# A two-layer decoder trunk in split float32 products: first loads from one queue, squares summed on VectorE, another order for the output product's last units, and a scale spread by two float32r products

## The chip, the cores and the metric

The kernel runs on one core of one Trainium2 chip, in one launch. The metric is the device time of one execution in microseconds (us). Three executions of the kernel before took 1090.64 to 1091.21 us, the median 1091.2.

## What is computed

The input is one sequence of 512 positions with 1024 features, in float32. Two layers follow each other. Each has a token mixer and a gated MLP, both behind an RMSNorm, both added to the residual `h`:

```python
def rmsnorm(x, g):
    y = xf * lax.rsqrt(jnp.mean(xf * xf, axis=-1, keepdims=True) + RMS_EPS)
    return y * g
# layer 0: z = gelu(h @ w_in); u, v = split(z); v = layernorm(v);
#          s = causal 128x128 mixing of v in each chunk + b_s;   mix = (u * s) @ w_out
# layer 1: q, k, v, f_logit = split(h @ w_qkvf); causal softmax attention in 16 heads of 64,
#          logits + cumulative log-sigmoid forget gates;         mix = o @ w_o
# both:    a = conv_b + causal depthwise conv3(h @ w_gate);  h + (silu(a) * (h @ w_up)) @ w_down
# last:    rmsnorm(h, final_norm_g)
```

The weights are about 90 MB of float32 and are read once.

## The kernel before

**Units.** All weights lie in memory as units of 128 x 1024 float32 (512 KB), in the order of use. `fetch` (lines 75 to 83) asks SP for the next unit into one of three `raw` buffers and calls `split` (lines 110 to 113): ACT casts the unit to float32r, the high half `whi` (line 112), and DVE subtracts that from the unit, the low half `wlo` (line 113). There are two buffers each of `whi` and `wlo`. `unit(depth)` keeps up to `depth` units fetched ahead and hands out the oldest. Activations are split in the same way into `x` or `z` pairs.

**Products.** A block of 128 x 128 weights by 512 positions is three float32r matrix products into one PSUM bank (`triple`, lines 165 to 169: high by high, high by low, low by high). A unit is 8 blocks, so 24 products. PSUM has eight banks: two each under the tags g, s, a and b. The kernel is one stream of such products on PE; a tile scheduler has set each engine's order from the order in which the code is written, and within an engine instructions run in that order.

**Norms.** `norm_split` (lines 115 to 130) scales a 128-feature block of `h` by the norm's weight and splits it, so the products can begin before the norm's scale is known. `norm_square` (lines 132 to 141) squares the block on ACT and adds the square to a running sum on POOL (line 141). `norm_end` sums over partitions by four one-column products (line 148), takes the inverse root on DVE with three Newton steps (lines 96 to 108) on a 128 x 4 tile, and multiplies the identity by each of its columns into a 128 x 512 tile of four diagonals (line 152). `norm_spread` (line 159) multiplies that by a matrix of ones in plain float32, which spreads the scale to all partitions. This happens for four norms; the last norm of the kernel is done in another way in the tail.

**The start.** `build` first runs nine small float32 products of ones (line 742, 18 passes on PE), and loads the first weights from SP (lines 751 and 78) and the input `x` from ACT's queue (lines 745 to 754), so that ACT's first casts stand behind its own DMA instructions. The first unit is loaded and split in two pieces of 512 columns.

**The output product of the attention.** `wo` multiplies the attention's result (pairs `z`) by eight units of w_o, (group, half) = (0,0) (1,0) (2,0) (0,1) (1,1) (2,1) (3,0) (3,1). A group is two PSUM banks of 128 output features; the banks of the groups 0, 1, 2 are gg, ab, ss. Each half holds four blocks of 128 input features, and the last of these (two heads) is ready only when the attention ends. So the (0,1) and (1,1) units are held in the two `whi`/`wlo` buffers, all their products but those with the last block are issued, then the last ones, and the buffers come free for (2,1). After each group `add_to_h` adds its banks to `h` (line 216) and does the next norm's `norm_split` and `norm_square`. The attention's probabilities are split into three buffers with the tag `hl`.

Of the kernel before, what the change touches and what calls it, by code (L numbers as in the profile page):

```python
# [8 lines left out]
F32 = mybir.dt.float32  # L9
F32R = mybir.dt.float32r  # L10
# [3 lines left out]
ALU = mybir.AluOpType  # L14
AX = mybir.AxisListType

P = 128
T = 512
D = 1024
KD = D // P  # L20
# [3 lines left out]
NT = T // P  # L24
# [8 lines left out]
V_MIX = 0  # L33
# [9 lines left out]
class Trunk:  # L43
# [29 lines left out]


    def fetch(self):
        nc = self.nc
        raw = self.sb("raw", 3, [P, 1024])
        nc.sync.dma_start(out=raw, in_=self.ins["w"][self.iu])
        self.iu += 1
        hi = self.sb("whi", 2, [P, 1024], F32R)  # L80
        lo = self.sb("wlo", 2, [P, 1024], F32R)
        self.split(hi, lo, raw)
        self.ahead.append((hi, lo))

    def unit(self, depth=2):

# [45 lines left out]
    def norm_square(self, k):  # L132

        nc = self.nc
        if self.acc is None:
            self.acc = self.tmp()
            nc.scalar.activation(out=self.acc, in_=self.h[k], func=AF.Square)
        else:
            sq = self.tmp()
            nc.scalar.activation(out=sq, in_=self.h[k], func=AF.Square)  # L140
            nc.gpsimd.tensor_tensor(out=self.acc, in0=self.acc, in1=sq, op=ALU.add)  # L141

    def norm_end(self):

        nc = self.nc
        pt = self.ps("a")
        for i in range(NT):
            nc.tensor.matmul(pt[:, i : i + 1], self.acc[:, i * P : (i + 1) * P], self.ones[:, 0:1], start=True, stop=True)
        self.r4 = self.rsqrt(pt[:, 0:NT], NT, 1.0 / D, RMS_EPS)
        dg = self.tmp()  # L150
        for i in range(NT):
            nc.vector.tensor_scalar(out=dg[:, i * P : (i + 1) * P], in0=self.ident, scalar1=self.r4[:, i : i + 1],
                                    scalar2=None, op0=ALU.mult)
        self.dg = dg

    def norm_spread(self):
        nc = self.nc
        pb = self.ps("b")
        nc.tensor.matmul(pb, self.ones, self.dg, start=True, stop=True)
        self.R = self.sb("R", 1, [P, T])  # L160
        nc.scalar.copy(out=self.R, in_=pb)

# [200 lines left out]
    def fox(self):  # L363
        nc = self.nc
        V = [self.sb("v", 4, [P, H, P], F32R) for _ in range(NT)]
        self.V = V
        x = (self.xh, self.xl)

        wf3 = self.wfr.rearrange("p (k h) -> p k h", k=KD)
        self.wf = self.sb("pt", 3, [P, 1280], F32R)[:, 0:1024].rearrange("p (k c) -> p k c", k=KD)  # L370
        nc.gpsimd.memset(self.wf.bitcast(F32), 0.0)
        hi, lo = self.wf[:, :, 0:H], self.wf[:, :, H : 2 * H]
        nc.gpsimd.tensor_copy(out=hi, in_=wf3)
        nc.gpsimd.tensor_tensor(out=lo, in0=wf3, in1=hi.bitcast(F32), op=ALU.subtract)

        def each_v(g, kp):
            if g == 0 and kp == 2:
                self.norm_end()
            elif g == 0 and kp == 3:
                self.norm_spread()  # L380
                self.gates()
            elif g == 1 and kp == 1:
                self.running_sums()

        def evac_v(g, banks):
            for i in range(NT):
                r = self.r4[:, i : i + 1]
                src = banks[i].rearrange("p (h d) -> p h d", d=HD)
                vh, vl = V[i][:, 8 * g : 8 * g + 8, 0:HD], V[i][:, 8 * g : 8 * g + 8, HD:P]
                nc.scalar.activation(out=vh, in_=src, func=AF.Copy, scale=r)  # L390
                nc.vector.scalar_tensor_tensor(out=vl, in0=src, scalar=r, in1=vh.bitcast(F32), op0=ALU.mult, op1=ALU.subtract)

        self.gemm_tm(x, KD, 2, evac_v, each_v)

        self.oh, self.ol = [], []
        self.st, self.pr, self.hl, self.po = {}, {}, {}, {}

        def qk():
            for p in range(H // 2):
                st = self.stack_tiles(p)  # L400
                pq, pk = self.ps("g"), self.ps("g")
                for u in range(2):
                    hi, lo = self.unit()
                    for m, pt in enumerate((pq, pk)):
                        for j in range(4):
                            k = 4 * u + j
                            c = slice(j * 256 + m * P, j * 256 + (m + 1) * P)
                            self.triple(pt, (hi[:, c], lo[:, c]), (x[0][k], x[1][k]), k == 0, k == KD - 1)
                            if k == KD - 1:
                                (self.stack_k if m else self.stack_q)(p, pt, st)  # L410
                            yield

        def wo():

            y = (self.oh, self.ol)
            evac = self.add_to_h(V_FFN + 8, 2)
            banks = {}

            def blocks(g, unit, half, ks):
                hi, lo = unit  # L420
                for m in range(2):
                    for j in ks:
                        k = 4 * half + j
                        c = slice(j * 256 + m * P, j * 256 + (m + 1) * P)
                        self.triple(banks[g][m], (hi[:, c], lo[:, c]), (y[0][k], y[1][k]), k == 0, k == KD - 1)
                        yield

            for g, tags in enumerate(("gg", "ab", "ss")):
                banks[g] = [self.ps(tag) for tag in tags]
                yield from blocks(g, self.unit(), 0, range(4))  # L430
            held = []
            for g in range(2):
                held.append(self.unit(2 - g))
                yield from blocks(g, held[g], 1, range(3))
            for g in range(2):
                yield from blocks(g, held[g], 1, (3,))
                evac(g, banks[g])
            yield from blocks(2, self.unit(), 1, range(4))
            evac(2, banks[2])
            banks[3] = [self.ps("g") for _ in range(2)]  # L440
            for half in range(2):
                yield from blocks(3, self.unit(), half, range(4))
            evac(3, banks[3])

        def products():
            yield from qk()
            yield from wo()

        gen = products()
        for _ in range(20):
            next(gen)
        for slot in range(4 * H + LAG):
            for _ in range(2):
                next(gen)
            self.attend(slot)
        self.run(gen)
# [235 lines left out]

    def constants(self):
        nc = self.nc
        nc.gpsimd.affine_select(out=self.ident, in_=self.ones, pattern=[[1, P]], compare_op=ALU.is_equal, fill=0.0,
                                base=0, channel_multiplier=-1)
        nc.gpsimd.affine_select(out=self.tri, in_=self.ones, pattern=[[1, P]], compare_op=ALU.is_ge, fill=0.0,
# [4 lines left out]
                                base=0, channel_multiplier=1)  # L704
        nc.gpsimd.tensor_copy(out=self.identb, in_=self.ident)
        nc.gpsimd.tensor_copy(out=self.maskb, in_=mask)
        nc.sync.dma_start(out=self.wfr, in_=self.ins["wf"])
        nc.gpsimd.tensor_copy(out=self.fold, in_=self.ident[0 : 2 * H, 0:H])
        nc.gpsimd.tensor_tensor(out=self.fold, in0=self.fold, in1=self.ident[0 : 2 * H, H : 2 * H], op=ALU.add)
        self.cum = self.sb("cum", 1, [P, T], F32R)  # L710
# [4 lines left out]
    def build(self):  # L715
        nc, tc = self.nc, self.tc
        with tc.tile_pool(name="sb", bufs=1) as self.pool, \
                tc.tile_pool(name="ps", bufs=1, space=bass.MemoryType.PSUM) as self.psum:
            self.ones = self.sb("ones", 1, [P, P])
            self.ident = self.sb("ident", 1, [P, P])  # L720
            self.tri = self.sb("tri", 1, [P, P])
            self.wfr = self.small(P, tag="wfr", bufs=1)
            self.vec = self.sb("vec", 1, [P, NV])
            self.identb = self.sb("identb", 1, [P, P], BF16)
            self.maskb = self.sb("maskb", 1, [P, P], BF16)
# [19 lines left out]
            nc.scalar.dma_start(out=self.vec, in_=self.ins["vec"])  # L745
            raw = self.sb("raw", 3, [P, 1024])
            hi, lo = self.sb("whi", 2, [P, 1024], F32R), self.sb("wlo", 2, [P, 1024], F32R)

            for j in range(2):
                c = slice(j * 512, (j + 1) * 512)  # L750
                nc.sync.dma_start(out=raw[:, c], in_=self.ins["w"][0, :, c])
                nc.scalar.dma_start(out=hb[0][:, j], in_=self.ins["x"][:, j])
            for q in range(1, KD // 2):
                nc.scalar.dma_start(out=hb[q], in_=self.ins["x"][:, 2 * q : 2 * q + 2])
            for j in range(2):
                c = slice(j * 512, (j + 1) * 512)
                self.split(hi[:, c], lo[:, c], raw[:, c])
                self.norm_split(j, V_MIX, 2)
            self.iu = 1
            self.ahead.append((hi, lo))  # L760
            self.fetch()
            for k in range(2, KD):
                self.norm_split(k, V_MIX)

            self.gmlp()
            self.run(self.gemm_fm((self.zh, self.zl), KE, 2, self.add_to_h(V_FFN)))
# [71 lines left out]
```

## Time and profile before

| | |
|---|---|
| median of three runs | 1091.2 us (1090.64 to 1091.21) |
| the profiled execution's own time | 1091.33 us |
| its span, first to last instruction | 1089.6 us |
| PE busy | 1074.4 us (99%), 5018 instructions |
| DVE, ACT, POOL busy | 622.1, 441.5, 70.4 us |
| mean granted TensorE clock | 0.994 of full speed |

The time of an execution is the span and a further 1.7 us around it. PE is the engine that bounds the kernel: a moment without a product, or with products at the lower of TensorE's two clock levels (1.2 GHz rather than 2.4 GHz), lengthens the span, while idle time on another engine costs nothing by itself. A matrix product's row shows its start and its pipelined duration (0.39 us); the next one starts 0.2275 us after it at full clock, and 0.43 us after it at the lower level, so the distance between starts is what counts.

### The profile page before, as it was taken

The numbers are of one execution on the slowest core, as the hardware profiler recorded it, in microseconds if no ns is written. First come the engines' busy times: TensorE is split into PE (matmuls) and PEld (weight loads), VectorE is DVE, ScalarE is ACT, GpSimd is POOL, SyncE is SP. The second block draws the span as 40 slices with busy tenths as digits, with TensorE's granted clock in tenths as the row PEclk, the third lists the DMA queues.
The fourth block names the chain that finished last, engine by engine and source line by source line (L and its number), as shares of the span: only waits on it lengthen the run. The fifth ranks groups of instructions, "written<-read, shape, count | busy, mean of one in ns | idle before, by whom it ended". The sixth has DMA issues, their size and how long they took to land.

```text
span 1089.6 us, 12928 instructions
## 1 busy us (share of the span) xinstructions
PE 1074.4 (99%) x5018; PEld 885.5 (81%) x5018; DVE 622.1 (57%) x1007; ACT 441.5 (41%) x706; POOL 70.4 (6%) x62
## 2 busy tenths in 40 slices
PE   8999999999999999999999999999989999999997
PEld 7878888888888888888887888877768888888886
DVE  5535856534555665545254699999564655655242
ACT  6332333322333433333133577777442433433232
POOL 5000000001200000001020010110030000000000
PEclk9999999999999999999999999999989999999999
DMA  6222222222223222222222211111122223232222
GB/s 257 96 79 96 93 82 78 96 98 96 98 78 97 97 97 97 99 96 98 97 96 83 98 61 41 60 62 59 59 78 97 95 97 98 78 116 78 97 97 78
DMA packets 28669, 99.44 MB, mean 91 GB/s; under 512 B 3456, under 2 KB 3712, under 8 KB 28608
## 3 DMA queue, kind: packets, MB, share of 16 engines
q1 hardware_dynamic: 27744, 96.42, 25.7%
q10 hardware_dynamic: 864, 2.20, 0.5%
q8 instruction: 39, 0.64, 0.2%
q14 instruction: 22, 0.18, 0.1%
HBM read 96.12 MB, written 2.10 MB: 90 GB/s over the span
## 4 chain that ended last, share of the span: by engine, by line
PE 89%; DVE 7%; ACT 2%; DMA 1%; issue 1%; ACTq 0%; DVEq 0%
PE psg L167 11%; PE psg L168 11%; PE psg L169 11%; PE pss L169 9%; PE pss L167 9%; PE pss L168 9%; PE psa L167 4%; PE psa L168 4%; PE psa L169 4%; PE psb L167 4%; PE psb L168 4%; PE psb L169 4%; DVE wlo L113 2%; DVE hl L113 1%; DVE z L545 1%; PE psa L590 1%
## 5 line engine op out<-in xcount | busy, mean ns | idle before, releaser
L113 DVE TENSOR_TENSOR wlo<-raw,whi 128x1024 fp32r<-128x1024 f32 (+1 forms) x173 | 219.6, 1269 | 371.4 <-ACT whi L112 359.2
L112 ACT CAST whi<-raw 128x1024 fp32r<-128x1024 f32 (+1 forms) x173 | 180.8, 1045 | 453.0 <-PE psg L168 132.2
L167 PE MATMUL psg<-x,whi 128*128 128x512 f32 x336 | 136.1, 405 | 0.0
L169 PE MATMUL psg<-x,wlo 128*128 128x512 f32 x336 | 131.3, 391 | 0.0
L168 PE MATMUL psg<-x,whi 128*128 128x512 f32 x336 | 130.9, 390 | 0.0
L167 PE MATMUL pss<-x,whi 128*128 128x512 f32 x192 | 75.9, 395 | 0.0
L168 PE MATMUL pss<-x,whi 128*128 128x512 f32 x192 | 74.7, 389 | 0.0
L169 PE MATMUL pss<-x,wlo 128*128 128x512 f32 x192 | 74.7, 389 | 0.0
L169 PEld LDWEIGHTS psg<-x,wlo 128*128 128x128 f32 x336 | 63.1, 188 | 13.5
L167 PEld LDWEIGHTS psg<-x,whi 128*128 128x128 f32 x336 | 63.9, 190 | 11.1
L141 POOL TENSOR_TENSOR tmp<-tmp,tmp 128x512 f32<-128x512 f32 x28 | 47.0, 1678 | 399.8 <-ACT tmp L140 398.5
L168 PEld LDWEIGHTS psg<-x,whi 128*128 128x128 f32 x336 | 63.3, 188 | 11.2
L167 PE MATMUL psg<-z,whi 128*128 128x512 f32 x128 | 50.3, 394 | 0.6 <-ACT z L112 0.6
L169 PE MATMUL psg<-z,wlo 128*128 128x512 f32 x128 | 50.0, 391 | 0.0
L168 PE MATMUL psg<-z,whi 128*128 128x512 f32 x128 | 49.8, 389 | 0.0
L169 PE MATMUL pss<-z,wlo 128*128 128x512 f32 x112 | 44.8, 402 | 3.7 <-DVE wlo L113 3.7
L167 PE MATMUL psa<-x,whi 128*128 128x512 f32 x120 | 47.3, 394 | 0.0
L169 PE MATMUL psa<-x,wlo 128*128 128x512 f32 x120 | 46.7, 389 | 0.0
L168 PE MATMUL psa<-x,whi 128*128 128x512 f32 x120 | 46.7, 389 | 0.0
L167 PE MATMUL psb<-x,whi 128*128 128x512 f32 x120 | 46.7, 389 | 0.0
L169 PE MATMUL psb<-x,wlo 128*128 128x512 f32 x120 | 46.7, 389 | 0.0
L168 PE MATMUL psb<-x,whi 128*128 128x512 f32 x120 | 46.7, 389 | 0.0
(282 smaller groups left out, 2221.7 us busy)
## 6 DMA issues: line engine op xcount, KB each, us to landing
raw<-w SPq DMA_DIRECT2D x175, 512.0 KB
out<-v SPq DMA_DIRECT2D x8, 256.0 KB
h<-x ACTq DMA_DIRECT2D x3, 512.0 KB
raw<-w SPq DMA_DIRECT2D x2, 256.0 KB
h<-x ACTq DMA_DIRECT2D x2, 256.0 KB
pt<-ws SPq DMA_DIRECT2D x1, 512.0 KB
pt<-bs SPq DMA_DIRECT2D x1, 512.0 KB
z<-cum SPq DMA_DIRECT2D x32, 8.0 KB
```

The costliest lines, as they stand in the source:

```text
L112: nc.scalar.copy(out=hi, in_=src)
L113: nc.vector.tensor_tensor(out=lo, in0=src, in1=hi.bitcast(F32), op=ALU.subtract)
L141: nc.gpsimd.tensor_tensor(out=self.acc, in0=self.acc, in1=sq, op=ALU.add)
L167: self.nc.tensor.matmul(out, ah, bh, start=start, stop=False)
L168: self.nc.tensor.matmul(out, ah, bl, start=False, stop=False)
L169: self.nc.tensor.matmul(out, al, bh, start=False, stop=stop)
L545: nc.vector.tensor_tensor(out=bk[0:HD], in0=f[own], in1=ak[own].bitcast(F32), op=ALU.subtract)
L590: nc.tensor.transpose(pt[:, (qi - kb) * P : (qi - kb + 1) * P], pr[:, o : o + P], self.ident)
```

## The change

- The first loads all go out from SP, in this order: the first half of the first unit, `x` block 0 in two halves of 256 positions, the second half of the unit, `x` block 1, `x` blocks 2 and 3, the second unit, and the rest of `x`. ACT issues only the small `vec` (norm weights). Block 1 is split in one piece rather than two.
- `norm_square` adds on DVE, not POOL: 28 instructions, seven for each of four norms.
- `norm_end` splits the 128 x 4 scale into a float32r high and low part and makes four diagonals of each, and `norm_spread` multiplies both by ones in float32r into one bank. A float32r tile of ones is new.
- In `wo`, the (0,1) and (1,1) units are fetched together; (1,1) is split into two `hl` buffers. Two more fetches, of (2,1) and (3,0), are written in ahead of the places at which `unit` would have asked for them.
- The small load of the forget-gate weights moves from the start into `fox`, into a `tmp` buffer.

```diff
     def fetch(self):
-        nc = self.nc
+        self.ahead.append(self.fetch_into([self.sb(tag, 2, [P, 1024], F32R) for tag in ("whi", "wlo")]))
+
+    def fetch_into(self, parts):
         raw = self.sb("raw", 3, [P, 1024])
-        nc.sync.dma_start(out=raw, in_=self.ins["w"][self.iu])
+        self.nc.sync.dma_start(out=raw, in_=self.ins["w"][self.iu])
         self.iu += 1
-        hi = self.sb("whi", 2, [P, 1024], F32R)
-        lo = self.sb("wlo", 2, [P, 1024], F32R)
-        self.split(hi, lo, raw)
-        self.ahead.append((hi, lo))
+        self.split(*parts, raw)
+        return parts
...
-            nc.gpsimd.tensor_tensor(out=self.acc, in0=self.acc, in1=sq, op=ALU.add)
+            nc.vector.tensor_tensor(out=self.acc, in0=self.acc, in1=sq, op=ALU.add)
...
         self.r4 = self.rsqrt(pt[:, 0:NT], NT, 1.0 / D, RMS_EPS)
-        dg = self.tmp()
-        for i in range(NT):
-            nc.vector.tensor_scalar(out=dg[:, i * P : (i + 1) * P], in0=self.ident, scalar1=self.r4[:, i : i + 1],
-                                    scalar2=None, op0=ALU.mult)
-        self.dg = dg
+        rh, rl = (self.small(NT, F32R) for _ in range(2))
+        self.split(rh, rl, self.r4)
+        self.dg = [self.tmp(F32R) for _ in range(2)]
+        for dg, r in zip(self.dg, (rh, rl)):
+            for i in range(NT):
+                nc.vector.tensor_scalar(out=dg[:, i * P : (i + 1) * P], in0=self.ident, scalar1=r[:, i : i + 1].bitcast(F32),
+                                        scalar2=None, op0=ALU.mult)
...
-        nc.tensor.matmul(pb, self.ones, self.dg, start=True, stop=True)
+        for q in range(2):
+            nc.tensor.matmul(pb, self.onesr, self.dg[q], start=q == 0, stop=q == 1)
...
-            held = []
+            held = [self.unit(1), self.fetch_into([self.sb("hl", 3, [P, 1024], F32R) for _ in range(2)])]
             for g in range(2):
-                held.append(self.unit(2 - g))
                 yield from blocks(g, held[g], 1, range(3))
+            self.fetch()
             for g in range(2):
                 yield from blocks(g, held[g], 1, (3,))
+                if g == 0:
+                    self.fetch()
                 evac(g, banks[g])
...
             for j in range(2):
                 c = slice(j * 512, (j + 1) * 512)
                 nc.sync.dma_start(out=raw[:, c], in_=self.ins["w"][0, :, c])
-                nc.scalar.dma_start(out=hb[0][:, j], in_=self.ins["x"][:, j])
-            for q in range(1, KD // 2):
-                nc.scalar.dma_start(out=hb[q], in_=self.ins["x"][:, 2 * q : 2 * q + 2])
-            for j in range(2):
-                c = slice(j * 512, (j + 1) * 512)
+                for q in range(2 - j):
+                    t = slice(q * T // (2 - j), (q + 1) * T // (2 - j))
+                    nc.sync.dma_start(out=hb[0][:, j, t], in_=self.ins["x"][:, j, t])
                 self.split(hi[:, c], lo[:, c], raw[:, c])
-                self.norm_split(j, V_MIX, 2)
+                self.norm_split(j, V_MIX, 2 - j)
             self.iu = 1
             self.ahead.append((hi, lo))
-            self.fetch()
-            for k in range(2, KD):
-                self.norm_split(k, V_MIX)
+            for q in range(1, KD // 2):
+                nc.sync.dma_start(out=hb[q], in_=self.ins["x"][:, 2 * q : 2 * q + 2])
+                if q == 1:
+                    self.fetch()
+                self.norm_split(2 * q, V_MIX)
+                self.norm_split(2 * q + 1, V_MIX)
```

Three places show how the order of instructions moves. The first is SP's queue at the start; here `raw_96` is the first unit, `h` the input. Before:

```order
L751 DMA raw_96<-w 128x512 x2
L78 DMA raw_122<-w 128x1024
L78 DMA raw_194<-w 128x1024
L707 DMA wfr_4_64<-wf 128x128
L713 DMA bf_9_69<-bf 128x16
L319 DMA pt_519<-ws 128x1024
L321 DMA pt_521<-bs 128x1024
L78 DMA raw_230<-w 128x1024
```

The same place on SP after the change:

```order
L757 DMA raw_96<-w 128x512
L760 DMA h_20_91<-x 128x256 x2
L757 DMA raw_96<-w 128x512
L760 DMA h_20_91<-x 128x512
L766 DMA h_21_92<-x 128x1024
L80 DMA raw_121<-w 128x1024
L766 DMA h_22_93<-x 128x1024
L766 DMA h_23_94<-x 128x1024
L80 DMA raw_195<-w 128x1024
```

The input stands between the weights in one queue, and the second unit now follows the second piece of `h`, the third unit all of it.

The second place is PE at the end of the attention in `wo`. `z_6458` and `z_6459` are the high and low halves of the last attention result, `whi_6294` is the unit (0,1), `whi_6388` (1,1) and `whi_6513` (2,1); psg, psa, psb, pss are the banks. Before, around the first product with the last result:

```order
L168 MATMUL psb_6175<-z_6310,whi_6388 128x512
L169 MATMUL psb_6175<-z_6309,wlo_6389 128x512
L167 MATMUL psg_6055<-z_6458,whi_6294 128x512
L167 MATMUL psg_6056<-z_6458,whi_6294 128x512
L167 MATMUL psa_6174<-z_6458,whi_6388 128x512
L167 MATMUL psb_6175<-z_6458,whi_6388 128x512
L168 MATMUL psg_6055<-z_6459,whi_6294 128x512
L169 MATMUL psg_6055<-z_6458,wlo_6295 128x512
```

After, at the same place, where `z_6489` is the last result's high half, `hl_6417` and `hl_6418` the unit (1,1) and `whi_6499` the unit (2,1):

```order
L172 MATMUL psb_6206<-z_6340,hl_6418 128x512
L170 MATMUL pss_6321<-z_5856,whi_6499 128x512
L171 MATMUL pss_6321<-z_5857,whi_6499 128x512
L172 MATMUL pss_6321<-z_5856,wlo_6500 128x512
L170 MATMUL pss_6321<-z_6105,whi_6499 128x512
L171 MATMUL pss_6321<-z_6106,whi_6499 128x512
L170 MATMUL psg_6086<-z_6489,whi_6323 128x512
L170 MATMUL psg_6087<-z_6489,whi_6323 128x512
L170 MATMUL psa_6205<-z_6489,hl_6417 128x512
L171 MATMUL psg_6086<-z_6490,whi_6323 128x512
```

Five products of the unit (2,1) now stand ahead of the first that needs the last result.

The third place is DVE behind the attention's end, where `h_20`, `h_21` and `h_22` are the residual's blocks. Before:

```order
L113 TENSOR_TENSOR z_6459<-tmp_6400,z_6458 128x512
L216 TENSOR_TENSOR h_20_91<-psg_6055,h_20_91 128x512
L216 TENSOR_TENSOR h_20_91<-psg_6056,h_20_91 128x512
L216 TENSOR_TENSOR h_21_92<-psa_6174,h_21_92 128x512
L127 SCALAR_TENSOR_TENSOR x_6476<-h_20_91,vec_65,x_6475 128x512
L216 TENSOR_TENSOR h_21_92<-psb_6175,h_21_92 128x512
L127 SCALAR_TENSOR_TENSOR x_6481<-h_20_91,vec_65,x_6480 128x512
L113 TENSOR_TENSOR wlo_6514<-raw_6511,whi_6513 128x1024
```

After the change, on DVE from the same instruction on:

```order
L113 TENSOR_TENSOR z_6490<-tmp_6431,z_6489 128x512
L219 TENSOR_TENSOR h_20_91<-psg_6086,h_20_91 128x512
L219 TENSOR_TENSOR h_20_91<-psg_6087,h_20_91 128x512
L113 TENSOR_TENSOR wlo_6512<-raw_6513,whi_6511 128x1024
L127 SCALAR_TENSOR_TENSOR x_6519<-h_20_91,vec_65,x_6518 128x512
L141 TENSOR_TENSOR tmp_6527<-tmp_6527,tmp_6529 128x512
L127 SCALAR_TENSOR_TENSOR x_6524<-h_20_91,vec_65,x_6523 128x512
L219 TENSOR_TENSOR h_21_92<-psa_6205,h_21_92 128x512
```

Before, the low half of (2,1) is made after all four bank sums. After, that half was made before the attention's end, and the low half here (`wlo_6512`) is that of (3,0); the sums of squares (line 141) stand among the rest.

## Rows read from the trace of the kernel before

**Rows 1.** The page's line of engines: busy time, share of the span, instructions of each engine

```profile
PE 1074.4 (99%) x5018; PEld 885.5 (81%) x5018; DVE 622.1 (57%) x1007; ACT 441.5 (41%) x706; POOL 70.4 (6%) x62
```

**Rows 2.** PE's waits: engine, line, waited for, us in total, times, longest

```profile
PE pss L169 <- DVE wlo L113: 3.7, 1, 3.7
```

**Rows 3.** Windows: busy of PE, PEld, DVE, ACT, POOL; granted clock, DMA share, GB/s

```profile
0.00:4.00 4.00, 2.94 (x14) 2.94 (x15) 0.00 (x0) 1.49 (x2) 2.00 (x11) 1.00 0.49 154
4.00:8.00 4.00, 2.11 (x9) 1.57 (x9) 1.43 (x4) 1.94 (x4) 0.00 (x0) 1.00 0.98 354
8.00:12.00 4.00, 4.00 (x12) 3.10 (x12) 3.29 (x6) 3.12 (x6) 0.00 (x0) 0.57 1.03 407
...
788.00:792.00 4.00, 3.40 (x15) 2.48 (x14) 1.75 (x3) 1.27 (x3) 0.00 (x0) 1.00 0.00 0
...
800.00:804.00 4.00, 4.00 (x11) 3.10 (x11) 2.98 (x3) 0.76 (x2) 0.60 (x1) 0.56 0.25 76
```

**Rows 4.** Timeline of the start: start, duration in us, instruction [idle before <- releaser]

```profile
1.06 4.05 PE L742 MATMUL psb<-ones 128*128 128x128 f32 x18 [1.06 <-POOL ones L736]
3.98 1.90 ACTq L754 DMA_DIRECT2D h<-x  x2
5.92 0.62 ACT L112 CAST whi<-raw 128x512 fp32r<-128x512 f32 x1 [3.18 <-DMA h<-x]
6.45 0.90 ACT L126 ACTIVATE x<-h,vec 128x256 fp32r<-128x256 f32 x2
7.00 0.50 PE L167 MATMUL psg<-whi,x 128*128 128x512 f32 x1 [1.89 <-ACT x L126]
11.70 0.39 PE L167 MATMUL psg<-whi,x 128*128 128x512 f32 x1
19.90 0.39 PE L167 MATMUL psg<-whi,x 128*128 128x512 f32 x1
20.51 0.50 PE L168 MATMUL psg<-wlo,x 128*128 128x512 f32 x1 [0.22 <-DVE wlo L113]
```

**Rows 5.** The chain that ended last, its pieces in the start

```profile
2.21 8.49 DMA h<-x
```

**Rows 6.** Timeline of PE where the attention ends, in `wo`

```profile
788.93 0.40 PE L169 MATMUL psb<-z,wlo 128*128 128x512 f32 x1
789.93 0.73 PE L167 MATMUL psg<-z,whi 128*128 128x512 f32 x2 [0.60 <-ACT z L112]
...
797.84 0.80 PE L169 MATMUL pss<-z,wlo 128*128 128x512 f32 x1 [3.68 <-DVE wlo L113]
...
803.55 0.40 PE L169 MATMUL pss<-z,wlo 128*128 128x512 f32 x1
```

**Rows 7.** Timeline of DVE there, of one DVE row at 295 us, and of POOL

```profile
791.62 1.29 DVE L216 TENSOR_TENSOR h<-psg,h 128x512 f32<-128x512 f32 x2 [1.02 <-PE psg L169]
793.56 0.75 DVE L127 SCALAR_TENSOR_TENSOR x<-h,vec,x 128x512 fp32r<-128x512 f32 x1
795.49 2.30 DVE L113 TENSOR_TENSOR wlo<-raw,whi 128x1024 fp32r<-128x1024 f32 x1
...
295.81 1.23 DVE L113 TENSOR_TENSOR wlo<-raw,whi 128x1024 fp32r<-128x1024 f32 x1 [0.20 <-ACT whi L112]
...
795.32 5.29 POOL L141 TENSOR_TENSOR tmp<-tmp,tmp 128x512 f32<-128x512 f32 x3 [45.60 <-ACT tmp L140]
```

**Rows 8.** Timeline of PE around the first norm's spread

```profile
48.95 1.02 PE L159 MATMUL psb<-tmp,ones 128*128 128x512 f32 x2
...
50.05 0.39 PE L168 MATMUL psa<-wlo,x 128*128 128x512 f32 x1
```

**Rows 9.** Timeline of the second norm: diagonals and spread

```profile
309.82 0.88 DVE L152 TENSOR_SCALAR tmp<-ident,sm 128x128 f32<-128x128 f32 x4
311.98 1.02 PE L159 MATMUL psb<-tmp,ones 128*128 128x512 f32 x2
```

**Rows 10.** Timeline after the first norm's inverse root

```profile
37.18 1.27 ACT L253 ACTIVATE v<-psg,sm 128x512 f32<-128x512 f32 x2 [4.62 <-DVE sm L108]
```

More of the change, by code (lines that the diff above doesn't have):

```diff
@@ L367, in fox @@
         x = (self.xh, self.xl)
-        wf3 = self.wfr.rearrange("p (k h) -> p k h", k=KD)
+        wfr = self.tmp()[:, 0:P]
+        nc.sync.dma_start(out=wfr, in_=self.ins["wf"])
+        wf3 = wfr.rearrange("p (k h) -> p k h", k=KD)
         self.wf = self.sb("pt", 3, [P, 1280], F32R)[:, 0:1024].rearrange("p (k c) -> p k c", k=KD)
@@ L696, in constants @@
         nc = self.nc
+        nc.gpsimd.tensor_copy(out=self.onesr, in_=self.ones)
         nc.gpsimd.affine_select(out=self.ident, in_=self.ones, pattern=[[1, P]], compare_op=ALU.is_equal, fill=0.0,
@@ L706, in constants @@
         nc.gpsimd.tensor_copy(out=self.maskb, in_=mask)
-        nc.sync.dma_start(out=self.wfr, in_=self.ins["wf"])
         nc.gpsimd.tensor_copy(out=self.fold, in_=self.ident[0 : 2 * H, 0:H])
@@ L719, in build @@
             self.ones = self.sb("ones", 1, [P, P])
+            self.onesr = self.sb("onesr", 1, [P, P], F32R)
             self.ident = self.sb("ident", 1, [P, P])
             self.tri = self.sb("tri", 1, [P, P])
-            self.wfr = self.small(P, tag="wfr", bufs=1)
             self.vec = self.sb("vec", 1, [P, NV])
```

## The prediction, made before the changed kernel ran

> **What bounds the kernel now.** I began with the line of busy times [rows 1]: PE is busy 99% of the span, so only what stands on PE's path can move the time: a wait, an extra pass, or a stretch at the lower clock. PE's waits [rows 2] are few, one of them 3.7 us. The windows [rows 3] give the clock: it is full but for 0.57 between 8 and 12 us and 0.56 between 800 and 804 us, two stretches that each follow a wait of PE. Then the timelines: the start [rows 4] and the end of the attention [rows 6, 7] hold nearly all time that PE loses; the four spreads [rows 8, 9] hold a little. In the chain that ended last, one input piece is on the path for 8.49 us from its issue [rows 5].
>
> The sum is made against the profiled execution, 1091.33 us (span 1089.6 and 1.7 around it), 0.1 above the median of 1091.2.
>
> **The start.** Before, ACT is in its own DMA instructions until 5.88 (3.98 + 1.90), and only then casts the first piece and scales block 0 (6.45 to 7.35); the first real product starts at 7.00, 1.89 after the warming products end at 5.11 [rows 4]. The clock then falls: twelve products with block 0 take 7.00 to 11.70, 4.70 us against 12 x 0.2275 = 2.73. From 11.70 a further 12 products and unit 1 (24 x 0.2275 = 5.46) reach unit 2 at 19.90, where a late low half costs (20.51 - 19.90) - 0.2275 = 0.38.
>
> After, when does the input land? The windows show what the DMA engines delivered [rows 3]: 4 us x 154 GB/s = 0.62 MB by 4 us, 354 KB per us to 8 us, 407 after, with a DMA share of 0.98 and 1.03, so they are full and only the order can change. Checked on the row of before: block 2 lands at 2.21 + 8.49 = 10.70 [rows 5]; ahead of or between its packets lie some 2.8 MB (the first unit, units 1 and 2, the first four blocks, vec, the forget weights), which the curve gives at 9.9, so I add 0.8 for the completion. In the new order the running sums are 0.36 MB (vec and the first piece), 0.62 (block 0), 0.88, 1.15 (block 1), 1.67 (blocks 2, 3), 2.20 (unit 1), 2.72, 3.24, 3.77 (unit 2). That gives block 0 at 4.8, block 1 at 6.3, blocks 2 and 3 at 7.8, unit 1 at 9.2, unit 2 at 13.1. ACT scales block 0 in 0.90 [rows 4], so the first product starts near 5.7. PE has then been idle for 0.6; the trace has a wait of 0.60 at 789.93 [rows 6] with a window at full clock around it [rows 3], so I let the clock stay. Block 0 ends at 5.7 + 2.73 = 8.4, block 1 at 11.2. Unit 1 needs its cast and its low half: 9.2, the cast near 1.1 behind what ACT is in (to 10.7) and 1.23 on DVE [rows 7] bring 11.95; the second product wants it at 11.4, so 0.5 is lost. Unit 2 begins at 11.2 + 0.5 + 5.46 = 17.2 against 19.90, and the 0.38 goes with the collision described below: 3.1 gained. With landings as early as the curve without the 0.8 it is 3.9; I take 3.4. Bounds: no gain at all if ACT's and SP's queues matter less than I think, 4.1 if PE never stops after 5.11.
>
> On this the Trainium skill has two rules in "DMA: Bandwidth & Descriptors". "Issuing engines are not separate DMA queues" says that spreading transfers over engines saves only issue time; the full DMA share of the rows agrees, and by it the loss of ACT's queue costs nothing here. Its section "Bandwidth" gives 0.95 us for 64 KB and 6.15 for 1 MB and speaks against cutting block 0 in two: an estimate from these two figures is 1.3 us for each half and 2.0 for the whole, 0.6 more; by that the sum would lose 0.6. No row here shows a transfer of that size.
>
> **Squares on DVE.** 28 sums leave POOL. On DVE one costs what its neighbours of the same shape do, 1.29 / 2 = 0.65 [rows 7], 28 x 0.65 = 18 us of DVE time. What it takes away: while POOL's three sums run from 795.32, the low half of a unit takes 2.30 on DVE, elsewhere 1.23 [rows 7]. For a norm's burst of four sums the added 2.6 is paid by about two such slowed instructions at 1.07 each and the slower x splits. PE doesn't wait for DVE in the two other bursts now, and units are 5.46 apart, so I cost the edit at nothing, between -0.4 (the stall at 20.51 counted already) and a wait of about 2 at a burst. If the cover goes, what is late next is the unit's low half.
>
> **The spread.** From 48.95 to 50.05 lie two passes of the ones product and one ordinary product [rows 8]: 1.10 - 0.2275 = 0.87 for the spread. Two float32r products at 0.2275 take 0.455. That is 0.41 off each, four times 1.65. The added chain is a cast of 128x4, a subtraction and a second set of diagonals (0.88 [rows 9]). The first set ends at 309.82 + 0.88 = 310.70 and PE reaches the spread at 311.98 [rows 9]; with about 0.4 for the two small ones and 0.88, the second set is there near 312.0, the second product wants it at 312.2. ACT is idle there. So nothing is lost, by a margin of 0.2. In the first norm the small cast stands on ACT ahead of the gelu of 37.18 that frees a bank [rows 10], for which PE waits: minus 0.2. Bounds: 0 (four late second sets) to 1.65.
>
> **The end of the attention.** Before [rows 6]: the product at 788.93 is followed at 789.93, 1.00 - 0.23 = 0.77 lost; then 3.68 on the low half of unit (2,1); then thirteen products from 797.84 to 803.55 at the lower clock, 5.71 - 13 x 0.2275 = 2.75. Together 7.2, with some tenths more for the unit's late high half; I take 7.4. The low half is late since `whi` and `wlo` free up only when the last result's products are done, and it then stands on DVE behind four bank sums, two x splits and POOL's collision (791.62 to 797.79) [rows 7]. After, (2,1) has both halves made before the attention ends, since (1,1) lives in `hl`: five of its products fill the first 0.77 (5 x 0.23 = 1.1), and the rest runs on behind. What is late next? The low half of unit (3,1): between the first bank sum and it DVE has six bank sums and four sums of squares at 0.65, five x splits at some 0.67 and two low halves at about 1.14, 12.1 us; PE has 55 products, 12.5 us, until it needs it. It fits by 0.4. The `hl` buffers left to the attention's last step are one instead of three, which puts its splits one after another; the distances on PE (four products, 0.9) are near a split's own time, and I allow 0.2. So 7.2 is gained, between 2.5 (the clock falls again on a new wait) and 7.7.
>
> The forget weights' load in `fox` finds an idle queue; nothing.
>
> **Sum.** 3.4 + 1.65 - 0.2 + 7.2 = 12.05; 1091.33 - 12.05 = 1079.3, on the median's footing 1079.2.
>
> **Rivals.**
> - A, the forecast: 1079.2; its own range, from the start's 1.9 to 4.1 and tenths elsewhere, is 1077.5 to 1080.8. Chance 0.60.
> - B, the start stays: block 0 comes late, PE idles near two microseconds after its warming products and the clock falls as before. For it: the input in smaller pieces and one queue. Against: the full DMA engines [rows 3] and ACT no longer in its DMA instructions until 5.88. Some 0.5 remains of 3.4: 1082.1. Chance 0.14.
> - C, the wait in `wo` moves to (3,0) or (3,1): DVE's 12.1 against 12.5 is a thin margin. Priced as the start's wait: 1.89 and 4.70 - 2.73 = 1.97 of slow clock, 3.9: 1083.1. Chance 0.12.
> - D, slower: the sums on DVE push the low halves behind each norm's evacuation past PE's need, as the one at 797.84 is now: 3.68 + 2.75 = 6.4 each. There are three such bursts beside the start: with two, 1079.2 + 12.8 = 1092.0, no change; with three, 1098.4. For it: DVE has no long gap from 791.62 to 797.79 [rows 7]. Against: the sums before slowed DVE by nearly as much. It decides where the burst costs DVE over 2 us net. Chance 0.09, of it 0.05 for three.
> - E, the edit of the spread doesn't do what it says: float32r products of ones are no cheaper, or their second diagonals come late: 1.65 lost, 1080.9. Chance 0.05.
>
> **How the numbers follow.** A measurement of this kernel tells about 0.2%, 2.2 us, from no change. A, B, C and E are all faster by more, 0.91; two waits of D are the same, 0.04; three are slower, 0.05. The range leaves out D and the best of A's tail: 1077.0 to 1084.2.
>
> **What would show it.** Right: the first real product before 6.2 and no clock below full in the windows to 16 us; unit 2 near 17; no wait for `wlo` after the attention and full clock from 796 to 804; spreads with two products 0.23 apart; low halves near 1.23 throughout. Wrong: a wait of PE on `x` or `h` in the start, on `wlo` in the last group of `wo`, on the second diagonal at a spread, or behind an evacuation. Above 1084 two terms failed; above 1091 it is D.

## The result and the profile after

The changed kernel takes 1080.86 us (median of five runs, 1080.58 to 1080.89); the kernel before, 1091.2 in the same five rounds. The ratio is 0.9906, 95% interval 0.9891 to 0.992: faster by 10.3 us. The forecast was 1079.2, so the time lies in the range, 1.7 us above the forecast: 12.0 us were forecast, 10.3 came.

The line of engines, to be held against [rows 1]:

```profile
PE 1068.5 (99%) x5018; PEld 882.0 (82%) x5018; DVE 621.4 (58%) x1054; ACT 442.7 (41%) x709; POOL 26.8 (2%) x35
```

POOL has lost 43.6 us of work and DVE has gained none: the 28 sums (19 us on DVE) and the second diagonals (4.4) are paid by low halves and `x` splits that no longer run beside POOL (10 and 11 us less).

PE's waits after the change; the 3.7 of [rows 2] is gone. These two are in the start; the others are 1.2 us in six pieces in the attention and 1.1 ahead of the warming products, both as before, and two of 0.2:

```profile
PE psg L170 <- ACT whi L112: 1.2, 1, 1.2
PE psg L170 <- ACT x L126: 0.3, 1, 0.3
```

Windows of the start and of the end of the attention (busy of PE, PEld, DVE, ACT, POOL; granted clock, DMA share, GB/s), for [rows 3]:

```profile
4.00:8.00 4.00, 4.00 (x18) 3.13 (x17) 2.18 (x4) 2.89 (x6) 0.00 (x0) 1.00 0.86 247
8.00:12.00 4.00, 3.51 (x13) 2.10 (x12) 2.42 (x4) 2.75 (x6) 0.00 (x0) 1.00 1.01 407
...
800.00:804.00 4.00, 4.00 (x20) 3.24 (x19) 3.71 (x5) 1.52 (x3) 0.00 (x0) 1.00 0.39 133
```

Both stretches at half clock are gone. But between 4 and 8 us the DMA engines moved 247 GB/s, not the 354 of before.

The timeline of the start, for [rows 4]:

```profile
4.16 0.97 SPq L766 DMA_DIRECT2D h<-x  x2
5.08 0.50 PE L170 MATMUL psg<-whi,x 128*128 128x512 f32 x1
7.68 0.72 ACT L126 ACTIVATE x<-h,vec 128x512 fp32r<-128x512 f32 x1 [1.09 <-DMA h<-x]
8.45 0.50 PE L170 MATMUL psg<-whi,x 128*128 128x512 f32 x1 [0.27 <-ACT x L126]
10.18 0.72 ACT L126 ACTIVATE x<-h,vec 128x512 fp32r<-128x512 f32 x1 [1.25 <-DMA h<-x]
11.94 1.03 ACT L112 CAST whi<-raw 128x1024 fp32r<-128x1024 f32 x1
13.02 0.74 PE L170 MATMUL psg<-whi,x 128*128 128x512 f32 x2 [1.19 <-ACT whi L112]
18.96 0.39 PE L170 MATMUL psg<-whi,x 128*128 128x512 f32 x1
```

The first real product starts at 5.08 (5.7 was forecast), right behind the warming products. Then the input is late: ACT scales block 1 at 7.68 and block 2 at 10.18 as they land, where 6.3 and 7.8 were forecast. Unit 1 starts at 13.02, behind a cast that stands in ACT's queue after the scaling of blocks 2 and 3, and unit 2 at 18.96 instead of 19.90.

The end of the attention, for [rows 6]; the third row is the first product with the last result, the fourth the low half of unit (2,1), the last the low half of unit (3,1):

```profile
787.33 0.40 PE L170 MATMUL pss<-z,whi 128*128 128x512 f32 x1
787.57 0.40 PE L171 MATMUL pss<-z,whi 128*128 128x512 f32 x1
787.80 0.62 PE L170 MATMUL psg<-z,whi 128*128 128x512 f32 x2
...
790.58 0.39 PE L172 MATMUL pss<-z,wlo 128*128 128x512 f32 x1
...
801.23 0.40 PE L172 MATMUL psg<-z,wlo 128*128 128x512 f32 x1
```

```profile
790.48 1.22 DVE L113 TENSOR_TENSOR wlo<-raw,whi 128x1024 fp32r<-128x1024 f32 x1
...
799.81 1.22 DVE L113 TENSOR_TENSOR wlo<-raw,whi 128x1024 fp32r<-128x1024 f32 x1
```

PE doesn't stop: products start 0.23 apart from one end to the other. The second fence is DVE: the low half that was feared to be late ends at 801.03, 0.2 us before PE wants it (0.4 was forecast), and takes 1.22 rather than the 2.30 of [rows 7]. The spread, for [rows 8], is two products in 0.48:

```profile
47.63 0.64 PE L162 MATMUL psb<-tmp,onesr 128*128 128x512 f32 x2
48.11 0.40 PE L170 MATMUL psa<-whi,x 128*128 128x512 f32 x1
```

**Where the 10.4 us of the two profiled executions (1091.33 and 1080.89) come from.** PE runs 5018 instructions in both, so the same place in its stream has a start in each, and the difference grows at a few places only (the 0.48 is read at the tenth product of unit 2, which starts at 22.46 before and 21.04 after):

| place | forecast | measured |
|---|---|---|
| start, to unit 2 (19.90 - 18.96), and the low half of unit 2 | 3.4 | 0.94 + 0.48 = 1.42 |
| bank wait after the first inverse root | -0.2 | -0.08 |
| four spreads | 1.65 | 0.35 + 0.37 + 0.40 + 0.37 = 1.49 |
| end of the attention | 7.2 | 7.8 |
| last store, issue to end (3.06 before, 3.24 after) | 0 | -0.18 |
| sum | 12.05 | 10.45 |

### The profile page after: what moved, and what is told of

Same layout as the page of the kernel before. It is cut to its first block, busy times and chain, and to the rows that moved or that the text cites. A ratio compares the mean times of both kernels' runs of the same rounds, so it can differ in the third digit from the quotient of the medians.

```text
span 1079.2 us, 12934 instructions
## 1 busy us (share of the span) xinstructions
PE 1068.5 (99%) x5018; PEld 882.0 (82%) x5018; DVE 621.4 (58%) x1054; ACT 442.7 (41%) x709; POOL 26.8 (2%) x35
## 3 DMA queue, kind: packets, MB, share of 16 engines
q1 hardware_dynamic: 28608, 98.52, 26.4%
## 4 chain that ended last, share of the span: by engine, by line
PE 87%; DVE 7%; ACT 1%; issue 1%; DVEq 0%; ACTq 0%
PE psg L170 11%; PE psg L171 10%; PE psg L172 10%; PE pss L170 9%; PE pss L171 9%; PE pss L172 9%; PE psa L170 4%; PE psb L170 4%; PE psa L171 4%; PE psb L171 4%; PE psa L172 4%; PE psb L172 4%; DVE wlo L113 1%; DVE hl L113 1%; DVE z L552 1%; DVE sm L583 1%
## 5 line engine op out<-in xcount | busy, mean ns | idle before, releaser
L113 DVE TENSOR_TENSOR wlo<-raw,whi 128x1024 fp32r<-128x1024 f32 (+1 forms) x172 | 209.3, 1217 | 365.3 <-ACT whi L112 353.1
L170 PE MATMUL pss<-z,whi 128*128 128x512 f32 x112 | 43.9, 392 | 0.0
L585 ACT ACTIVATE pt<-pss,sm 128x128 f32<-128x128 f32 (+1 forms) x64 | 33.9, 529 | 24.5 <-DVE sm L583 24.3
```

Source lines behind the costliest of these rows:

```text
L113: nc.vector.tensor_tensor(out=lo, in0=src, in1=hi.bitcast(F32), op=ALU.subtract)
L170: self.nc.tensor.matmul(out, ah, bh, start=start, stop=False)
L585: nc.scalar.activation(out=row, in_=s[:, 0:w], func=AF.Exp, bias=nm, accum_out=sm)
```

## The experiments

All are edits of the changed kernel. They ran in three sets; beside them the kernel before had medians of 1090.71, 1091.04 and 1090.62 us, against 1091.2 beside the changed kernel, so a difference of half a microsecond between sets says nothing. The first five ask why the start gave 1.4 and not 3.4. The two theories: transfers queued behind a piece are served beside it ("shared"), or one queue with this sequence delivers less than two ("rate").

**The old start, all else changed.** The block of `build` that issues the loads is that of before.

> The changed kernel with the start of before (the input again from ACT's queue, first unit's pieces and the next units from SP, block 1 split in two); everything else changed. Theory 'the order of the loads gave little': the start's share of the gain is the 0.94 us by which unit 2 began earlier, and up to 1.42 with what follows it, so 1081.8 to 1082.3 us, first real product at 7.0, clock 0.5 to 0.6 from 8 to 12 us. Rival (the prediction's own term): 3.4 us, so 1084.3.

Measured: 1084.22 us (1083.57 to 1084.59), 3.4 slower than the changed kernel. That is the number of the rival, the prediction's own term, but by luck: it came about in a way that neither had in mind. ACT's queue and SP's in its trace:

```profile
4.07 4.49 ACTq L760 DMA_DIRECT2D h<-x  x2
...
4.24 0.33 SPq L720 DMA_DIRECT2D bf<-bf  x1
5.41 0.33 SPq L322 DMA_DIRECT2D pt<-ws  x1
5.78 0.43 SPq L324 DMA_DIRECT2D pt<-bs  x1
```

ACT stands in its DMA instructions until 8.56, against 5.88 in [rows 4], and the first real product waits until 9.69. What differs from the kernel before is SP's queue: the load of the forget weights is gone from it, and the constants ws and bs (512 KB each) go out at 5.41 and 5.78.

**The same with the constants held back** until the input is split, by a copy of one column on POOL into their buffers:

```diff
+        nc.gpsimd.tensor_copy(out=wraw[:, 0:1], in_=self.xl[7][:, T - 1 : T].bitcast(F32))
         nc.sync.dma_start(out=wraw, in_=self.ins["ws"])
...
```

> The kernel with the old start again (1084.2 us, first product at 9.69), but the two constants of 512 KB (ws and bs) held back until the last block of the input is split. Theory: with the small load of the forget weights gone from SP's queue the constants went out at 5.41 and 5.78 instead of 8.01 and 8.39 and took the DMA engines from the input, and ACT stood in its DMA instructions until 8.56 instead of 5.88; held back, the first product is at 7.5 or earlier, unit 2 before 20.3 and the time 1081.8 to 1082.6. Rival: the constants don't matter, ACT's DMA instructions again last past 8 us, time 1083.8 or more.

Measured: 1081.82 us (1081.36 to 1083.25).

```profile
3.96 2.35 ACTq L762 DMA_DIRECT2D h<-x  x2
6.35 0.62 ACT L112 CAST whi<-raw 128x512 fp32r<-128x512 f32 x1 [3.61 <-DMA raw<-w]
```

ACT is free at 6.31, the first product starts at 7.43, and 2.4 of the 3.4 us are back. Unit 2 came later than expected (21.2), in a profile that is 1.4 us slower than the median: its products ran 0.43 apart until 13.15, since the clock had not risen yet (see the last section). The theory is right in its cause and wrong in its way: the constants did not delay the input's first blocks (the traces' completion events have block 1 at 8.61 in both kernels, blocks 2 and 3 at 10.87 and 10.83), but with them in SP's queue ACT's DMA instructions last 4.49 us rather than 2.35, and its first casts stand behind those. The edits aren't additive: against the old start as it would have become, the new one is worth 3.4 us; against an old start without that collision, 1.0.

**The followers held back:** unit 1, blocks 4 to 7, units 2 and 3 wait for block 0's split, in the same way, and the two constants for the input's last block.

```diff
+        if self.iu in (2, 3):
+            after = self.xl[0]
+        if after is not None:
+            self.nc.gpsimd.tensor_copy(out=raw[:, 0:1], in_=after[:, T - 1 : T].bitcast(F32))
         self.nc.sync.dma_start(out=raw, in_=self.ins["w"][self.iu])
...
```

> The changed kernel; the loads behind the input's blocks 2 and 3 (unit 1, blocks 4 to 7, units 2 and 3, and two constants) are held back until block 0 is split, near 6.1 us, by a one-column copy on POOL into their buffers. Theory 'shared': transfers queued behind a piece are served beside it, so that blocks 2 and 3 land only when 2.5 MB have come instead of the 1.67 MB ahead of and in them; held back, they land by 9.2 instead of 10.18 us (ACT's scaling of block 2 starts then). Rival 'rate': one queue is served in order and only slowly between 4 and 8 us (247 GB/s); the scaling still starts at 10.0 or later. The time itself may rise or fall by 0.5 us, since unit 1 is issued later.

Measured: 1081.81 us (1081.02 to 1083.5).

```profile
6.48 0.33 SPq L84 DMA_DIRECT2D raw<-w  x1
...
7.57 0.72 ACT L130 ACTIVATE x<-h,vec 128x512 fp32r<-128x512 f32 x1 [0.27 <-DMA h<-x]
8.83 0.72 ACT L130 ACTIVATE x<-h,vec 128x512 fp32r<-128x512 f32 x1
```

Block 2 is scaled at 8.83, just as it lands and ACT is free. "Shared" holds: with nothing behind them, blocks 2 and 3 come 1.35 us earlier than in the changed kernel's profile, and earlier than in any of the five traces whose start is the changed kernel's (scaled at 9.34 to 10.41). It does not pay. PE starts unit 1 at 12.20 rather than 13.02, but unit 2 at 18.33, and from unit 2's tenth product (20.96 against 21.04) on it is 0.1 us ahead: the low halves of both units hold PE up, the second until 19.70. They stand in DVE's queue, and DVE is busy in all 4.00 us from 16 to 20, here and in the changed kernel. So by these traces DVE is the next limit of the start behind the landings.

**Blocks 0 and 1 from ACT's queue,** issued ahead of its table load:

```diff
             nc.scalar.dma_start(out=self.vec, in_=self.ins["vec"])
+            for j in range(2):
+                for q in range(2 - j):
+                    t = slice(q * T // (2 - j), (q + 1) * T // (2 - j))
+                    nc.scalar.dma_start(out=hb[0][:, j, t], in_=self.ins["x"][:, j, t])
             warm = self.small(1)
...
```

> The changed kernel with the three pieces of the input's blocks 0 and 1 issued from ACT, right behind vec and ahead of its table load; all else of the start from SP. Theory 'rate': two queues fill the DMA engines between 4 and 8 us as before the change (354 GB/s against 247), block 1 is there by 6.9 instead of 7.68 and blocks 2 and 3 by 9.3; the time falls by 0.4 to 1.0 us, to 1079.9 to 1080.5. Theory 'shared': blocks 2 and 3 still at 10.0 or later, and the time within 0.3 of the changed kernel's 1080.86.

Measured: 1081.24 us (1080.73 to 1081.94), not faster.

```profile
4.00:8.00 4.00, 3.44 (x11) 2.75 (x11) 1.18 (x2) 1.53 (x4) 0.00 (x0) 1.00 1.02 370
```

```profile
7.68 0.51 ACT L126 ACTIVATE x<-h,vec 128x256 fp32r<-128x256 f32 x1 [1.90 <-DMA h<-x]
...
9.57 0.72 ACT L126 ACTIVATE x<-h,vec 128x512 fp32r<-128x512 f32 x1 [0.88 <-DMA h<-x]
```

Here "rate" is right in its premise: two queues move 370 GB/s between 4 and 8 us, where one moved 228 to 247 in the five traces with the changed kernel's start. But ACT's small pieces don't profit: the second half of block 0 is scaled at 7.68 and block 1 (the last row) only at 9.57. Blocks 2 and 3, on SP's queue and issued at 1.71, land at 7.16, three microseconds earlier than in the changed kernel, and must wait in ACT's order for block 1. So SP's large transfers are served beside ACT's small ones and end first: both effects are there.

**Block 0 in one piece** of 256 KB.

> The changed kernel with the input's block 0 loaded in one piece of 256 KB rather than two of 128 KB. Theory 'small pieces are slow': the rate between 4 and 8 us rises above 247 GB/s, block 1 lands 0.3 us or more earlier than 7.68 and the time falls by some tenths. Otherwise: the first product is later than 5.08 by up to 0.4, landings unchanged, the time within 0.3 of 1080.86.

Measured: 1080.5 us (1080.26 to 1080.67); 271 GB/s between 4 and 8 us. First product at 5.60, unit 2 at 18.62. The rate is higher, but block 1 is scaled at 8.64, not earlier than 7.68, so "small pieces are slow" is not borne out. Cutting block 0 gained nothing that the next units kept; the 0.36 us are less than two profiles of one program differ by (below). The second half of the cut block lands between 4.62 and 6.23 in the five traces with the changed kernel's start, the whole block by 5.04 and 4.72 in two, so the 0.6 that the prediction set beside its sum for the cut is neither shown nor excluded.

**The sums of squares back on POOL.** One word of `norm_square`.

> The changed kernel with the 28 sums of squares back on POOL. The prediction's step (the move costs and gives nothing beside the 0.4 at unit 2): 1080.6 to 1081.7, with the low halves of 128x1024 beside POOL's sums at 2.3 us again, and perhaps a wait for a low half in the last group of the output product. Rival 'sums on DVE cost': faster than 1080.2. Rival 'the collision was worth more': a wait of 1 us or more on a low half and 1083 or more.

Measured: 1084.25 us (1083.95 to 1085.16; the profiled execution is the slowest), 3.4 slower: the rival that the collision was worth more. DVE, POOL and PE in its trace:

```profile
14.03 6.02 DVE L127 SCALAR_TENSOR_TENSOR x<-h,vec,x 128x512 fp32r<-128x512 f32 x4
19.97 3.51 DVE L113 TENSOR_TENSOR wlo<-raw,whi 128x1024 fp32r<-128x1024 f32 x2
...
14.81 6.36 POOL L141 TENSOR_TENSOR tmp<-tmp,tmp 128x512 f32<-128x512 f32 x4
...
22.31 0.50 PE L171 MATMUL psg<-wlo,x 128*128 128x512 f32 x1 [2.40 <-DVE wlo L113]
```

While POOL adds, four x splits take 6.02 us, 1.5 each instead of 0.75; the low half of unit 2 comes after them, PE waits 2.40 for it, and the next products run 0.43 apart to 26.4. All of it is in the start: unit 2's third block is 4.1 behind the changed kernel, that stays to the end, and at no other norm do the sums make PE wait.

**The output product's units fetched and held as before,** the sums still on DVE.

> The changed kernel with the output product's units held and fetched as before; the sums of squares stay on DVE. Theory 'buffers' (the prediction's): the low half of unit (2,1) is late because its buffers come free late, so a wait of 2 us or more on it and a stretch of half clock come back: 1085.5 to 1088.7. Rival 'collision': it was late because POOL's sums slowed DVE; with the sums on DVE the wait is under 1 us and the clock stays: 1081.0 to 1083.0.

Measured: 1088.62 us (1087.97 to 1090.72), 7.8 slower. The profiled execution, one of the slowest, loses 8.5 at this place and 1.0 in the start.

```profile
795.75 1.03 ACT L112 CAST whi<-raw 128x1024 fp32r<-128x1024 f32 x1
...
796.84 0.80 PE L170 MATMUL psg<-z,whi 128*128 128x512 f32 x1 [4.28 <-ACT whi L112]
797.43 0.63 PE L171 MATMUL psg<-z,whi 128*128 128x512 f32 x1
797.86 0.63 PE L170 MATMUL psg<-z,whi 128*128 128x512 f32 x1
```

The wait comes back, 4.28 us, though POOL is silent: in this order PE stops at unit (3,0)'s high half, because its cast stands behind the evacuation in ACT's queue, and unit (2,1)'s low half follows at 797.03 on DVE. Products 0.43 apart follow the wait, to 802.3. So the collision is not needed for the wait; the holding of the units is the cause. The `hl` buffers and the places of the two fetches were undone together, and which of them does how much is not shown. In [rows 2] the wait named DVE, since unit (2,1)'s low half was asked for first.

**The scale spread by one float32 product again.**

> The changed kernel with the scale spread by one float32 product again. By the two traces each spread gives 0.37 to 0.40 us: 4 x 0.38 = 1.5, so 1082.2 to 1082.6, the spread's products 0.43 apart. Rival 'no cheaper, the second diagonals cost what is won': 1080.7 to 1081.2.

Measured: 1081.77 us (1081.64 to 1082.49), 0.9 slower; between the two profiles the spans differ by 1.6.

```profile
47.78 1.02 PE L159 MATMUL psb<-tmp,ones 128*128 128x512 f32 x2
48.24 0.80 PE L167 MATMUL psa<-whi,x 128*128 128x512 f32 x1
48.88 0.39 PE L168 MATMUL psa<-wlo,x 128*128 128x512 f32 x1
```

From 47.78 to 48.88, less one ordinary product, the spread takes 1.10 - 0.23 = 0.87 us, against 0.48 in the changed kernel. In the two traces the four spreads cost 0.37 us each, 1.5 together, so the rival (no cheaper) falls. The median moved by less, and lies in neither range; why is open.

**The changed kernel once more, and three attempts at the start.**

> The changed kernel unaltered, once more, beside the next three on the same chip. 1080.5 to 1081.0 us; it shows how far the landings of the first loads differ between two executions of one program: the traces of kernels whose start is the same have unit 2 between 18.96 and 19.96.

Measured: 1080.61 us (1080.3 to 1081.16). In this profile block 2 is scaled at 9.65 and unit 2 starts at 18.43; in the first it was 10.18 and 18.96. So much in the start is chance from one profile to the next, and more: the three variants that leave the start's loads alone (sums on POOL, the units as before, the old spread) have block 1 scaled at 7.71, 9.02 and 9.04 and block 2 at 9.34, 10.26 and 10.41.

> The changed kernel with block 0 loaded whole and the squares of the input's blocks 1 to 3 made to wait for unit 1's cast (a one-column copy on POOL from it), so that ACT scales blocks 1 to 3 and casts unit 1 before it squares. Theory 'ACT's order': unit 1's cast ends up to 1.2 us earlier, unit 2 begins near 18.0 instead of 18.62 with block 0 whole, 1079.6 to 1080.3. Rival 'landing': unit 1 itself lands only shortly before its cast, which then waits for the load; 1080.3 to 1080.9.

Measured: 1081.6 us (1081.21 to 1081.64), slower, by 1.1 than with block 0 whole alone. The wait is not in the forecast of either theory:

```profile
11.19 1.05 ACT L112 CAST whi<-raw 128x1024 fp32r<-128x1024 f32 x1
...
18.31 0.77 DVE L143 TENSOR_TENSOR tmp<-tmp,tmp 128x512 f32<-128x512 f32 x1
19.01 1.31 DVE L113 TENSOR_TENSOR wlo<-raw,whi 128x1024 fp32r<-128x1024 f32 x1
```

Unit 1's cast is earlier (11.19), but the squares that it passed stand later in DVE's queue, and unit 2's low half ends at 20.3; PE reaches the place after it 0.6 us later than in the changed kernel (20.94 against 20.36).

> Block 0 whole, and unit 1, blocks 4 to 7, units 2 and 3 held back until the first piece is cast (near 4.6 instead of 6.1), the constants until the input is split. Theory 'shared': blocks 2 and 3 land by 9.0, unit 1 before 11, and unit 2 begins at 17.8 to 18.6 if PE's clock stays full, 1079.5 to 1080.5; with half clock on the first products as in the kernel that held them to 6.1, 1080.5 to 1081.5. Rival 'rate': as the changed kernel, 1080.5 to 1081.0.

Measured: 1080.63 us (1080.0 to 1080.97). Block 2 is scaled at 8.67 without a wait, as "shared" has it, but unit 1 lands only at 11.7 and PE waits 1.1 for its cast; unit 2 starts at 18.73. Between 4 and 8 us the one queue moves 335 GB/s here (334 in the next run). So the low rate of the changed kernel belongs to its sequence of loads and not to a single queue as such; what in the sequence lowers it no run separates.

> The two together: block 0 whole, the followers held until the first cast, the squares of blocks 1 to 3 behind unit 1's cast. If both the shared landings and ACT's order cost the forecast's 2 us, unit 2 begins near 17.5 and the time is 1078.8 to 1079.8; if neither does, 1080.5 to 1081.0.

Measured: 1081.0 us (1080.08 to 1081.48): unit 2 at 18.57, then the late low half as above. No order tried beats the changed kernel by more than its runs scatter.

## Why the prediction was right, and where its size was off

The signs of the three forecast gains held, and two of the three in size; the total was 1.7 us too good. The time, 1080.86, is that of rival E (1080.9), but by chance: E has the spread give nothing, and it gave 1.49. Undone one at a time, the start, the squares, the units and the spread cost 3.4 + 3.4 + 7.8 + 0.9 = 15.5 us, more than the 10.3 of the whole change: the gains don't add up.

- **End of the attention: right.** 7.2 forecast, 7.8 in the trace, and 7.8 lost in time when that edit alone is undone. The five products ahead of the last result fill the wait, and the low half of unit (3,1) is there 0.2 us early. The forecast had priced rival C at the right place: the margin is that thin.
- **Spread: right.** 1.65 forecast, 1.49 in the trace; undoing it costs 0.9 in time. The second diagonals make nobody wait.
- **Start: right sign, size wrong, 3.4 forecast and 1.42 measured.** The failing step is the landing curve: "the DMA engines ... are full and only the order can change". The forecast has block 1 at 6.3, blocks 2 and 3 at 7.8 and unit 1 at 9.2; in five traces with this start they land at 7.65 to 9.01, 9.31 to 10.38 and 10.61 to 11.67. The rate was not kept (228 to 247 GB/s for the 354 reckoned with; 370 with two queues, 335 with block 0 whole and the followers held), and the order in the queue was not the order of landing: block 2 was scaled at 10.18, when the windows give 0.62 + 0.99 + 2.18 us x 407 GB/s = 2.5 MB delivered instead of the 1.67 in and ahead of it, and earlier once its followers were held. The check of the curve on [rows 5] could hardly see this, since there too everything was under way at once; the 0.8 that it needed was booked as completion. Earlier landings of blocks 2 and 3 did not bring the missing 2 us back: with the followers held, low halves hold PE up instead, and the sum has no term for DVE's queue in the start beyond one low half. Of the signs named, the wait on `x` in the start came (0.3 us) and unit 2 near 17 did not. The short wait of PE with which the forecast let the clock stay at full did not arise: the first product follows the warming ones at once.
- **Squares on DVE: "I cost the edit at nothing" failed as a statement about the edit alone.** With the other edits in place it is worth 3.4 us, all in the start: with the new order the low half of unit 2 stands behind `x` splits that POOL's sums slow. The collision was seen in the rows [rows 7] and costed only where PE waited then.
- **Rival B** (the start stays) described half of what came: the clock did not fall, but most of the landing gain was missing. D is excluded: PE's waits name no low half.

## What to carry to other kernels

A start is a system: price a new order of loads by running sums only up to a bound, and allow that transfers queued behind a piece are served with it. An edit off the critical path may be what keeps another edit's gain, so cost it in the new order, not in the old. A DMA instruction can hold the engine that issues it (ACT for 1.90, 2.35 and 4.49 us here), so keep the first loads off the engine whose casts come first. Where PE waits for a half that is made of freed buffers, look for other buffers before looking for a faster engine.

## What the runs showed of the hardware beyond that

A window's granted clock of 1.00 is no reading where the trace has no record of the clock. The first record starts at 4.81 us in the kernel before, at 5.04 in the changed kernel and at 10.67 with blocks 0 and 1 on ACT's queue; ahead of it a window prints 1.00, that of 0 to 4 us in [rows 3] too. The distances between starts tell the level. The warming products are 0.21 apart, and with the units as before, where the record starts at 3.98, the last distances are 0.11: they run at the lower level until the clock rises. With blocks 0 and 1 on ACT's queue it had not risen when the first product began, so its products start 0.43 apart from 6.43 to 10.27, though the row of 4 to 8 us shown for it says 1.00. With the followers held the rise comes at 7.15, and with the old start and the constants held at 13.38; in the other traces it lies between 3.98 and 6.16. So slow first products need not mean that the clock fell; in the kernel before it did, from full to the lower level at 8.23, after the wait of 1.89 us.

Dropping a load of 64 KB from one queue kept the engine of the other queue in its DMA instructions 2.7 us longer (until 8.56, not 5.88), since the two 512 KB loads behind it went out 2.6 us earlier (8.01 before, 5.41 with the old start in the changed kernel). With these held back it was free at 6.31.
